# A down piece between the fourth and fifth seven-product pair, and third sums written over the raw words

## The chip, the cores and the metric

The kernel runs on one core of one Trainium2 chip. The metric is the device time of one execution in microseconds (us); lower is better. Engines are named as in the profile: PE (TensorE matmul), PEld (its weight load), DVE (VectorE), ACT (ScalarE), POOL (GpSimd) and SP (the queue that issues the loads here).

## The reference, cut to what matters

Two post-norm residual layers over 256 tokens of width 2048. Each layer has a mixer and a SwiGLU with 5632 hidden columns; the change lies in the SwiGLU alone.

```python
def swiglu(x, w_gate, w_up, w_down):
    return (jax.nn.silu(x @ w_gate) * (x @ w_up)) @ w_down
...
    for layer in range(DEPTH):
        ...
        x = layer_norm(DN_ALPHA * x + y, ln_mix_g[layer], ln_mix_b[layer])
        f = swiglu(x, ffn_w_gate[layer], ffn_w_up[layer], ffn_w_down[layer])
        x = layer_norm(DN_ALPHA * x + f, ln_ffn_g[layer], ln_ffn_b[layer])
```

## The kernel before

**Products.** Every float32 operand is split into a high part (a cast to float32r on ACT) and a low part (a subtraction on DVE); `mm3` then does three matmuls: low x high, high x high, high x low. The tokens are two tiles of 128. A matmul here is 128x128 times 128x512.

**SwiGLU.** The hidden columns are 11 chunks of 512. Chunks 0 and 1 are done by `whole`, the other nine by `unit`, so there are 9 units in a layer and 18 in all. For a unit, each of 8 weight pairs `w[p]` holds four blocks of 128x512 (two of gate, two of up). The four results of a unit, `c11`, `c12`, `c21`, `c22` (gate and up of the two token tiles), stand in four PSUM banks with the tag `un`.

- Three of the pairs (0, 1, 2) are multiplied plainly: two halves of 12 matmuls each.
- Five pairs (`SEVEN` = 3 to 7) are multiplied with seven block products in place of eight. Their left sides (`forms`, made once for a layer by `forms_of`) and their right sides are sums of blocks. `load_seven` loads a pair's four blocks as one 1 MB transfer into `raw` (tag `rs`, two buffers), makes two sums with the fourth block (the one operation that writes `z`), a third sum, and a fourth sum (`ze`, in a place called `room`), and splits block 0 and the first three sums into `sh` (high) and `sl` (low), two buffers each. A pair's four products at this stage are 12 matmuls.

**Order of a unit on PE.** It is written out by hand and pinned. First the unit before is finished: two "flips", each four transposes of one token tile of its result. Then the five seven-product pairs (`BEGIN` names the products and the results they go to), with `run(gap)` after each. Then ACT and DVE rework the four banks (the lines with `g0` and `g1` in `unit`: `c11` is copied, three differences are taken on DVE, and `c21` is written back by ACT with its sign changed). Then the remaining products, in the order `ORDER`: for pairs 3 to 7 three products each with `load_half` and the split of `edge` (`zf`); for pairs 0 to 2 two halves each. The first of these pieces is that of pair 3: three matmuls into `c11`, three into `c12`, three into `c21`.

**Down pieces.** `down_steps` is a generator of the down projection of two finished chunks. One step is one `load_half` (512 KB) and 12 matmuls into banks `acc`. A unit runs eight steps: in the kernel before, one ahead of each flip and one behind the second, then `GAPS` = 1, 1, 1, 0, 2 behind the five pairs.

**Order of everything else.** On DVE, ACT and the SP queue a scheduler decides at build time, from priorities (`tc.high_priority`) and its own estimates, in which order the instructions stand; each engine then runs its list in that order. Buffers: `whi`, `wlo` and `raw` of `load_half` have four each; `rs`, `sh`, `sl` have two each. A load into `rs` therefore waits until every reader of the pair two before has finished, and a cast into `sh` waits until PE has finished with the pair two before.

The two lines of the whole that the prediction uses most:

```python
raw = sp.tile([P, 4, NCH], F32, tag="rs", name="rs", bufs=2)
hi = sp.tile([P, 4, NCH], F32R, tag="sh", name="sh", bufs=2)
```

Of the kernel before, what the change touches and what calls it, by code (L numbers as in the profile page):

```python
# [11 lines left out]
F32 = mybir.dt.float32  # L12
# [6 lines left out]
P = 128  # L19
# [4 lines left out]
NCH = 512  # L24
# [46 lines left out]
ROUNDS = (((2, 3), (0, 1)), ((4, 5), (2, 3)), ((6, 7), (4, 5)), ((8, 9), (6, 7)), ((10,), (8,)))  # L71
LAST = (9, 10)
SEVEN = (3, 4, 5, 6, 7)
GAPS = (1, 1, 1, 0, 2)
ORDER = (3, 0, 4, 5, 1, 6, 7, 2)


# [1 line left out]
def trunk(ctx: ExitStack, tc: tile.TileContext, a, out):  # L79
    nc = tc.nc  # L80
    mult, add, sub = ALU.mult, ALU.add, ALU.subtract
# [15 lines left out]
    def bank(tag, bufs):  # L97
        return banks["pool"].tile([P, NCH], F32, tag=tag, name=tag, bufs=bufs)
# [22 lines left out]
    def split(hi, lo, src):  # L121
        nc.scalar.copy(hi, src)  # L122
        return nc.vector.tensor_tensor(lo, src, hi.bitcast(F32), op=sub).ins  # L123
# [53 lines left out]
    def half_done(n=1):  # L177
        for entry in list(later):
            entry[0] -= n
            if entry[0] <= 0:  # L180
                later.remove(entry)
                entry[1]()
# [95 lines left out]
    def split_tile(pool, shape, src, tag, bufs=1):  # L278
        hi = pool.tile(shape, F32R, tag=tag + "h", name=tag + "h", bufs=bufs)
        lo = pool.tile(shape, F32R, tag=tag + "l", name=tag + "l", bufs=bufs)  # L280
        if src is not None:
            split(hi, lo, src)
        return hi, lo

    def mm3(o, lhs, rhs, start, stop, pin=False, **more):

        for n, (a, b) in enumerate(((1, 0), (0, 0), (0, 1))):
            ins = nc.tensor.matmul(o, lhs[a], rhs[b], start=start and n == 0, stop=stop and n == 2, **more)  # L288
            if pin:
                tc.keep_in_program_order(ins)  # L290

    def at(pair, *ix):
        return pair[0][ix], pair[1][ix]
# [110 lines left out]
    def forms_of(sp, xT, out, seven, tag):  # L404

        n = len(seven)
        xs = sp.tile([P, NT, 2 * n, P], F32, tag="rs", name="xs", bufs=2)
        fs = sp.tile([P, 4, n, P], F32, tag="z", name="fs", bufs=1)
        yield
        for t in range(NT):  # L410
            s = slice(2 * seven[0], 2 * seven[0] + 2 * n)
            nc.vector.tensor_tensor(xs[:, t], xT[0][t][:, s, :].bitcast(F32), xT[1][t][:, s, :].bitcast(F32), op=add)
            yield
        x11, x12, x21, x22 = (xs[:, t, e : 2 * n : 2, :] for t in range(2) for e in range(2))
        e, f, g, h = (fs[:, i] for i in range(4))
        nc.vector.tensor_tensor(e, x22, x21, op=sub)
        nc.vector.tensor_tensor(f, e, x11, op=add)
        yield
        nc.vector.tensor_tensor(g, x11, x21, op=sub)
        nc.vector.tensor_tensor(h, x12, f, op=sub)  # L420
        yield
        hi, lo = split_tile(sp, [P, 4, n, P], fs, tag)
        for i, p in enumerate(seven):
            x = lambda t, k: (xT[0][t][:, k, :], xT[1][t][:, k, :])
            e, f, g, h = (at((hi, lo), slice(None), j, i) for j in range(4))
            out[p] = {"11": x(0, 2 * p), "12": x(0, 2 * p + 1), "22": x(1, 2 * p + 1), "e": e, "f": f, "g": g, "h": h}

    def load_seven(sp, src, room):

        with tc.high_priority(offset=400):  # L430
            raw = sp.tile([P, 4, NCH], F32, tag="rs", name="rs", bufs=2)
            hi = sp.tile([P, 4, NCH], F32R, tag="sh", name="sh", bufs=2)
            lo = sp.tile([P, 4, NCH], F32R, tag="sl", name="sl", bufs=2)
            z = sp.tile([P, 3, NCH], F32, tag="z", name="z", bufs=1)
            ze = room
            last_load[0] = nc.sync.dma_start(raw, src).ins
            nc.scalar.copy(hi[:, 0], raw[:, 0])
            nc.vector.tensor_tensor(z[:, :2], raw[:, 0:3:2], raw[:, 3:4].to_broadcast([P, 2, NCH]), op=add)
            nc.vector.tensor_tensor(z[:, 2], z[:, 0], raw[:, 2], op=add)  # L439
            nc.vector.tensor_tensor(ze, z[:, 2], raw[:, 1], op=add)  # L440
            nc.vector.tensor_tensor(lo[:, 0], raw[:, 0], hi[:, 0].bitcast(F32), op=sub)
            split(hi[:, 1:], lo[:, 1:], z)
        return lambda i: (hi[:, i, :], lo[:, i, :]), ze


    BEGIN = ((0, "11", "c11"), (3, "f", "c12"), (1, "e", "c22"), (2, "g", "c21"))

    def unit(sp, w, lhs, forms, y, down, flips):


        def run(n):
            for _ in range(n):
                next(down, None)

        for _ in range(NT):
            run(1)
            flips.pop(0)()
        run(1)
        b = {n: bank("un", 4) for n in ("c11", "c12", "c22", "c21")}
        edge, room = {}, None  # L460
        for i, (p, gap) in enumerate(zip(SEVEN, GAPS)):
            if i % 2:
                room = ap_.tile([P, 4, T], F32R, tag=("y4h", "y4l")[i // 2], name="ze4", bufs=1)
                room = room.rearrange("p (e a) t -> p e (a t)", e=2).bitcast(F32)
            own = room[:, (i + 1) % 2] if i else sp.tile([P, NCH], F32, tag="ze", name="ze", bufs=1)
            wt, edge[p] = load_seven(sp, w[p], own)
            for j, x, name in BEGIN:
                mm3(b[name], forms[p][x], wt(j), i == 0, i == len(SEVEN) - 1, True)
            if i == len(SEVEN) - 1:
                with tc.high_priority(offset=1000):  # L470
                    g0, g1 = (sp.tile([P, NCH], F32, tag=n, name=n, bufs=1) for n in ("g0", "g1"))
                    nc.scalar.copy(g0, b["c11"])
                    nc.vector.tensor_tensor(g1, b["c12"], g0, op=sub)
                    nc.vector.tensor_tensor(b["c12"], g1, b["c22"], op=sub)
                    nc.vector.tensor_tensor(g1, g1, b["c21"], op=sub)
                    nc.scalar.activation(b["c21"], g1, AF.Copy, scale=-1.0)
                    nc.vector.tensor_tensor(b["c22"], g1, b["c22"], op=sub)
            run(gap)

        left = {n: 2 * (8 - len(SEVEN)) + (n != "c22") * len(SEVEN) for n in b}  # L480

        def product(name, x, wt):
            left[name] -= 1
            mm3(b[name], x, wt, False, left[name] == 0, True, skip_group_check=True)

        for p in ORDER:
            if p in SEVEN:
                hi, lo = load_half(w[p][:, 1:3])
                for i, x, name in ((0, "12", "c11"), (1, "h", "c12")):
                    product(name, forms[p][x], (hi[:, i, :], lo[:, i, :]))  # L490
                with tc.high_priority(offset=400):
                    ends = split_tile(sp, [P, NCH], edge[p], "zf", 2)
                product("c21", forms[p]["22"], ends)
                half_done()
                continue
            for n, ks in ((0, (2 * p, 2 * p + 1)), (1, (2 * p + 1, 2 * p))):
                hi, lo = load_half(w[p][:, 2 * n : 2 * n + 2])
                for tok in range(NT):
                    for kk in range(2):
                        product(f"c{tok + 1}{n + 1}", lhs(tok, ks[kk]), (hi[:, kk, :], lo[:, kk, :]))  # L500
                half_done()
        with tc.high_priority(offset=1000):
            for tok in range(NT):
                g = sp.tile([P, NCH], F32, tag=f"g{tok}", name=f"g{tok}", bufs=1)
                nc.scalar.activation(g, b[f"c{tok + 1}1"], AF.Silu)
                nc.vector.tensor_tensor(g, g, b[f"c{tok + 1}2"], op=mult)
                s = slice(tok * P, (tok + 1) * P)
                flips.append(lambda g=g, s=s: transpose4(g, y[0][:, :, s], y[1][:, :, s], 1000))
# [35 lines left out]
    def ffn(layer, xT, res, mix_pool, close_mix, keep, last):  # L544
# [35 lines left out]
        forms, making, sps, flips = {}, [], [], []  # L580
# [10 lines left out]
        def change_rooms():  # L591
            close_mix()
            sps.append(later_pool(stack, f"sp{layer}"))
            making.append(forms_of(sps[0], xT, forms, SEVEN[:3], "fm"))
            making.append(forms_of(sps[0], xT, forms, SEVEN[3:], "fn"))
            later.append([1, make])

        groups = {c: None for c in range(2)}
# [498 lines left out]
    xT = new_xT()  # L1097
# [11 lines left out]
    def later_pool(stack, name):  # L1109
        return stack.enter_context(tc.tile_pool(name=name, bufs=1, reuse_waits="tile"))  # L1110
# [22 lines left out]
    xT = layer_end(0, a["ab_out"], AB_OUT_GROUPS, yT, False)  # L1133
# [117 lines left out]
```

## Time and profile before

| what | value |
|---|---|
| median of 3 runs | 2186.45 us (2184.64 to 2187.55) |
| the profiled execution's own time | 2190.12 us |
| its span in the profile | 2187.8 us |
| granted TensorE clock, mean | 0.997 |
| PE busy | 2148.9 us (98%), 9910 matmuls |
| DVE busy | 1691.1 us (77%) |
| ACT busy | 1215.7 us (56%) |
| read from HBM | 463.94 MB, 213 GB/s over the span |

The profile is of one execution. Durations in it are those of single instructions; matmuls overlap, so the distance from one matmul's start to the next one's is what a matmul costs, not the duration shown. In rows of the timeline the first number is the start in us from the start of the span, the second the duration in us, then engine, line and operation, output and inputs, and in brackets the idle time of the engine ahead of the instruction with what ended it. The 18 units lie at about 605 to 1180 us and 1560 to 2135 us.

### The profile page before, as it was taken

To read this page: it belongs to the slowest core of one execution; us is meant where nothing else is said; L and a number is where in the kernel's file an instruction comes from. 1 tells how busy PE (TensorE), PEld (TensorE's weight loads), DVE (VectorE), ACT (ScalarE), POOL (GpSimd) and SP (SyncE) were. 2 spreads that over 40 slices of the span, in tenths; PEclk is the share of its full clock that TensorE was granted. 3 is DMA by queue.
4 is the path that set the end of the run, shared out by engine and by line. 5 is a ranking of instruction groups with operands and counts; after the bars stand their busy time and mean duration, and the time that the engine had idled before them with its cause. 6 is when DMAs were issued, how large, how long until landed. Compare 5 with 4: busy or idle time off the path is not lost.

```text
span 2187.8 us, 27113 instructions
## 1 busy us (share of the span) xinstructions
PE 2148.9 (98%) x9910; PEld 1778.7 (81%) x9910; DVE 1691.1 (77%) x2122; ACT 1215.7 (56%) x1580; POOL 37.5 (2%) x43
## 2 busy tenths in 40 slices
PE   9999999999999999999999999999999999999998
PEld 7888888888878888888888788888788888888876
DVE  6886688676698888888886776675988888888866
ACT  6445534555455566666565554454556666565653
POOL 0000001000000000000000000000000000000000
PEclk9999999999999999999999999999999999999999
DMA  8555545684666776776665663655776766676754
GB/s 293 161 163 182 167 132 189 194 286 143 211 232 241 240 242 238 251 242 220 238 220 194 214 217 121 212 178 174 266 245 239 250 239 219 244 236 244 241 165 172
DMA packets 118613, 467.82 MB, mean 214 GB/s; under 512 B 13904, under 2 KB 16976, under 8 KB 105680
## 3 DMA queue, kind: packets, MB, share of 16 engines
q1 hardware_dynamic: 118480, 466.09, 63.0%
q8 instruction: 78, 1.28, 0.2%
q14 instruction: 55, 0.45, 0.1%
HBM read 463.94 MB, written 2.10 MB: 213 GB/s over the span
## 4 chain that ended last, share of the span: by engine, by line
PE 92%; DVE 3%; ACT 3%; DMA 1%; issue 0%; SPq 0%; ACTq 0%; DVEq 0%
PE acc L288 52%; PE un L288 30%; PE mx L288 6%; PE mx L803 1%; DVE sl L123 1%; PE tr L119 1%; ACT whi L122 1%; ACT sh L122 1%; PE un L119 1%; DVE wlo L123 1%; DMA raw<-in_cd_in 0%; ACT res L541 0%; DVE res L326 0%; DMA raw<-in_ab_in 0%; PE mx L849 0%
## 5 line engine op out<-in xcount | busy, mean ns | idle before, releaser
L123 DVE TENSOR_TENSOR wlo<-raw,whi 128x1024 fp32r<-128x1024 f32 (+1 forms) x671 | 814.7, 1222 | 321.2 <-ACT whi L122 311.8
L122 ACT CAST whi<-raw 128x1024 fp32r<-128x1024 f32 (+1 forms) x671 | 702.6, 1050 | 587.5 <-PE acc L288 302.5
L288 PE MATMUL acc<-whi,yTl 128*128 128x512 f32 x832 | 329.0, 396 | 1.2 <-DVE g L568 1.1
L288 PE MATMUL acc<-whi,yTh 128*128 128x512 f32 x832 | 325.0, 391 | 0.0
L288 PE MATMUL acc<-wlo,yTh 128*128 128x512 f32 x832 | 324.3, 391 | 0.0
L288 PE MATMUL acc<-whi,xTl 128*128 128x512 f32 x800 | 318.4, 398 | 5.2 <-ACT whi L122 5.1
L288 PE MATMUL acc<-whi,xTh 128*128 128x512 f32 x800 | 315.2, 394 | 0.0
L288 PE MATMUL acc<-wlo,xTh 128*128 128x512 f32 x800 | 313.0, 394 | 0.1
L288 PE MATMUL un<-whi,xTh 128*128 128x512 f32 x522 | 203.1, 389 | 0.0
L288 PE MATMUL un<-wlo,xTh 128*128 128x512 f32 x522 | 203.1, 389 | 0.0
L288 PE MATMUL un<-whi,xTl 128*128 128x512 f32 x522 | 203.1, 389 | 0.0
L288 PEld LDWEIGHTS acc<-whi,yTl 128*128 128x128 f32 x832 | 156.6, 188 | 33.6 <-DVE g L568 1.5
L288 PEld LDWEIGHTS acc<-wlo,yTh 128*128 128x128 f32 x832 | 156.6, 188 | 33.3
L288 PEld LDWEIGHTS acc<-whi,yTh 128*128 128x128 f32 x832 | 156.8, 188 | 31.4
L123 DVE TENSOR_TENSOR sl<-z,sh 128x1536 fp32r<-128x1536 f32 x90 | 157.9, 1755 | 29.4 <-ACT sh L122 28.9
L288 PEld LDWEIGHTS acc<-whi,xTl 128*128 128x128 f32 x800 | 151.1, 189 | 35.7 <-ACT whi L122 6.5
L122 ACT CAST sh<-z 128x1536 fp32r<-128x1536 f32 x90 | 133.3, 1481 | 81.3 <-DVE z L439 81.3
L288 PEld LDWEIGHTS acc<-wlo,xTh 128*128 128x128 f32 x800 | 150.9, 189 | 31.5 <-DVE wlo L123 1.2
L288 PEld LDWEIGHTS acc<-whi,xTh 128*128 128x128 f32 x800 | 151.2, 189 | 28.8
L288 PEld LDWEIGHTS un<-whi,xTh 128*128 128x128 f32 x522 | 98.0, 188 | 20.4
L288 PEld LDWEIGHTS un<-whi,xTl 128*128 128x128 f32 x522 | 98.0, 188 | 20.3
L288 PEld LDWEIGHTS un<-wlo,xTh 128*128 128x128 f32 x522 | 98.0, 188 | 20.3
(270 smaller groups left out, 3025.6 us busy)
## 6 DMA issues: line engine op xcount, KB each, us to landing
raw<-in_gu SPq DMA_DIRECT2D x262, 512.0 KB, 4.6
rs<-in_gu SPq DMA_DIRECT2D x90, 1024.0 KB, 6.9
raw<-in_down SPq DMA_DIRECT2D x176, 512.0 KB, 4.3
raw<-in_ab_in SPq DMA_DIRECT2D x127, 512.0 KB, 4.1
raw<-in_cd_in SPq DMA_DIRECT2D x40, 512.0 KB, 4.5
raw<-in_ab_out SPq DMA_DIRECT2D x32, 512.0 KB, 4.6
raw<-in_cd_out SPq DMA_DIRECT2D x32, 512.0 KB, 4.2
bias<-in_na_bias SPq DMA_DIRECT2D x32, 64.0 KB, 4.0
```

What stands on the lines that cost most here:

```text
L119: return nc.tensor.transpose(o, src, eye)
L122: nc.scalar.copy(hi, src)
L123: return nc.vector.tensor_tensor(lo, src, hi.bitcast(F32), op=sub).ins
L288: ins = nc.tensor.matmul(o, lhs[a], rhs[b], start=start and n == 0, stop=stop and n == 2, **more)
L803: nc.tensor.matmul(m[:, 2 * h + s, :], kk[:, h, s * P : (s + 1) * P], qq[:, h, r * P : (r + 1) * P], start=True, stop=True,)
```

## The change

- `GAPS` becomes 1, 1, 1, 1, 2: a down piece stands between the fourth and the fifth pair. To keep eight pieces in a unit, the piece between the two flips goes: one piece, both flips, one piece, then the pairs.
- In `load_seven` the third sum is written over block 2 of `raw`, so `z` holds two sums and gets two buffers (before: three sums, one buffer). High and low parts are made in two operations of 1024 columns each, one from blocks 0 and 2 of `raw`, one from `z` (before: 512 columns from `raw` and 1536 from `z`). The order of the four blocks in `sh` and `sl` changes, and `BEGIN` with it; the products are the same. The fourth sum (`room`) is the last in the code.
- The forms are made in three groups of 2, 2 and 1 pairs (before: 3 and 2), and their sums `fs` share the two buffers of `z`.

```diff
-GAPS = (1, 1, 1, 0, 2)
+GAPS = (1, 1, 1, 1, 2)
...
-        fs = sp.tile([P, 4, n, P], F32, tag="z", name="fs", bufs=1)
+        fs = sp.tile([P, 4, n, P], F32, tag="z", name="fs", bufs=2)
...
-            z = sp.tile([P, 3, NCH], F32, tag="z", name="z", bufs=1)
-            ze = room
+            z = sp.tile([P, 2, NCH], F32, tag="z", name="z", bufs=2)
             last_load[0] = nc.sync.dma_start(raw, src).ins
-            nc.scalar.copy(hi[:, 0], raw[:, 0])
-            nc.vector.tensor_tensor(z[:, :2], raw[:, 0:3:2], raw[:, 3:4].to_broadcast([P, 2, NCH]), op=add)
-            nc.vector.tensor_tensor(z[:, 2], z[:, 0], raw[:, 2], op=add)
-            nc.vector.tensor_tensor(ze, z[:, 2], raw[:, 1], op=add)
-            nc.vector.tensor_tensor(lo[:, 0], raw[:, 0], hi[:, 0].bitcast(F32), op=sub)
-            split(hi[:, 1:], lo[:, 1:], z)
-        return lambda i: (hi[:, i, :], lo[:, i, :]), ze
+            nc.vector.tensor_tensor(z, raw[:, 0:3:2], raw[:, 3:4].to_broadcast([P, 2, NCH]), op=add)
+            nc.vector.tensor_tensor(raw[:, 2], z[:, 0], raw[:, 2], op=add)
+            split(hi[:, :2], lo[:, :2], raw[:, 0:3:2])
+            split(hi[:, 2:], lo[:, 2:], z)
+            nc.vector.tensor_tensor(room, raw[:, 2], raw[:, 1], op=add)
+        return lambda i: (hi[:, i, :], lo[:, i, :]), room
...
-    BEGIN = ((0, "11", "c11"), (3, "f", "c12"), (1, "e", "c22"), (2, "g", "c21"))
+    BEGIN = ((0, "11", "c11"), (1, "f", "c12"), (2, "e", "c22"), (3, "g", "c21"))
...
+        run(1)
         for _ in range(NT):
-            run(1)
             flips.pop(0)()
         run(1)
...
-            making.append(forms_of(sps[0], xT, forms, SEVEN[:3], "fm"))
-            making.append(forms_of(sps[0], xT, forms, SEVEN[3:], "fn"))
+            for n, e in enumerate((2, 4, 5)):
+                making.append(forms_of(sps[0], xT, forms, SEVEN[2 * n : e], f"f{n}"))
```

The built order of the instructions shows more than the diff. First DVE, at the end of the five pairs of one unit in the middle of layer 0, before. `z<-rs` is the first two sums of a pair, `z<-z,rs` its third sum, `ze` its fourth; `sl` are low parts; `g` and `un` are the rework of the four banks (numbers behind a name are buffer numbers; lines are two higher before than after).

```order
L438 TENSOR_TENSOR z<-rs 128x1024
L473 TENSOR_TENSOR g_7997<-un,g_7996 128x512
L439 TENSOR_TENSOR z<-z,rs 128x512
L474 TENSOR_TENSOR un<-g_7997,un 128x512
L440 TENSOR_TENSOR ze<-z,rs 128x512
L475 TENSOR_TENSOR g_7997<-g_7997,un 128x512
L123 TENSOR_TENSOR sl<-z,sh 128x1536
L477 TENSOR_TENSOR un<-g_7997,un 128x512
```

One other instruction stands between each two of the rework; all belong to the next unit's first pair. The same place on DVE after the change (rework: L471, L472, L473, L475):

```order
L436 TENSOR_TENSOR z<-rs 128x1024
L123 TENSOR_TENSOR wlo<-raw,whi 128x1024
L471 TENSOR_TENSOR g_8009<-un,g_8008 128x512
L437 TENSOR_TENSOR rs<-z,rs 128x512
L123 TENSOR_TENSOR sl<-z,sh 128x1024
L472 TENSOR_TENSOR un<-g_8009,un 128x512
L436 TENSOR_TENSOR z<-rs 128x1024
L123 TENSOR_TENSOR wlo<-raw,whi 128x1024
L123 TENSOR_TENSOR sl<-rs,sh 128x1024
L473 TENSOR_TENSOR g_8009<-g_8009,un 128x512
```

The first `z<-rs` now belongs to the next unit's second pair, the second one to its third pair, and the rework stands behind them; the next unit's first pair is done ahead of this piece.

Second, ACT at the same place, before: the copy of `c11` into `g`, casts, and L476, which writes `c21`.

```order
L472 COPY g_7996<-un 128x512
L122 CAST sh<-z 128x1536
L437 CAST sh<-rs 128x512
L122 CAST whi<-raw 128x1024
L476 ACTIVATE un<-g_7997 128x512
```

And after, from the copy (L470) to the write of `c21` (L474):

```order
L470 COPY g_8008<-un 128x512
L522 ACTIVATE acc<-res_3803 128x512
L122 CAST sh<-z 128x1024
L122 CAST whi<-raw 128x1024
L122 CAST sh<-rs 128x1024
L539 COPY res_3802<-acc 128x512
L522 ACTIVATE acc<-res_3802 128x512
L122 CAST whi<-raw 128x1024
L539 COPY res_3803<-acc 128x512
L122 CAST whi<-raw 128x1024
L522 ACTIVATE acc<-res_3803 128x512
L474 ACTIVATE un<-g_8009 128x512
```

Ten instructions stand between the two where there were three; the last `whi` cast ahead of L474 is that of a piece behind the first one of `ORDER`.

Third, PE at the start of a unit, before: the transposes of the first flip with matmuls of a down piece on both sides.

```order
L288 MATMUL acc<-wlo,yTh 128x512
L119 MATMUL un<-ident,g_7729 128x128 x4
L288 MATMUL acc<-whi,yTl 128x512
L288 MATMUL acc<-whi,yTh 128x512
L288 MATMUL acc<-wlo,yTh 128x512
```

And after: both flips stand together.

```order
L288 MATMUL acc<-wlo,yTh 128x512
L119 MATMUL un<-ident,g_7741 128x128 x4
L119 MATMUL un<-ident,g_7744 128x128 x4
L288 MATMUL acc<-whi,yTl 128x512
L288 MATMUL acc<-whi,yTh 128x512
```

## The prediction

> **What bounds the kernel now.** I read the page first, then the list of waits of PE, then the timeline of single engines at a unit, then the loads.
>
> ```profile
> span 2187.8 us, 27113 instructions
> PE 2148.9 (98%) x9910; PEld 1778.7 (81%) x9910; DVE 1691.1 (77%) x2122; ACT 1215.7 (56%) x1580; POOL 37.5 (2%) x43
> ...
> PE un L288 <- DVE sl L123: 14.0, 18, 1.2
> ...
> PE un L288 <- DVE yTl L123: 2.2, 3, 0.8
> ```
>
> PE is the bound, so only what PE waits for can be won. The largest wait comes 18 times, once in a unit. PE's timeline shows the place, a fifth pair in layer 0:
>
> ```profile
> 1018.59 0.39 PE L288 MATMUL un<-sh,fnl 128*128 128x512 f32 x1
> 1018.82 0.39 PE L288 MATMUL un<-sh,fnh 128*128 128x512 f32 x1
> 1019.94 0.50 PE L288 MATMUL un<-sl,fnh 128*128 128x512 f32 x1 [0.73 <-DVE sl L123]
> 1020.27 0.40 PE L288 MATMUL un<-sh,fnl 128*128 128x512 f32 x1
> ```
>
> A matmul normally starts 0.227 us after the one before (1018.59 to 1018.82). Here one starts 1.12 later, 0.89 late, and the next 0.33 later, 0.10 late: 1.0 us is lost to the pair's low part. DVE at that time, and its next work (first numbers are starts):
>
> ```profile
> 1002.22 0.69 DVE L441 TENSOR_TENSOR sl<-rs,sh 128x512 fp32r<-128x512 f32 x1 [1.06 <-ACT sh L437]
> ...
> 1013.31 1.22 DVE L438 TENSOR_TENSOR z<-rs 128x1024 f32<-128x1024 f32 x1
> ...
> 1015.05 0.68 DVE L439 TENSOR_TENSOR z<-z,rs 128x512 f32<-128x512 f32 x1
> 1016.26 1.23 DVE L123 TENSOR_TENSOR wlo<-raw,whi 128x1024 fp32r<-128x1024 f32 x1 [0.52 <-ACT whi L122]
> 1017.40 0.68 DVE L440 TENSOR_TENSOR ze<-z,rs 128x512 f32<-128x512 f32 x1
> 1018.12 1.76 DVE L123 TENSOR_TENSOR sl<-z,sh 128x1536 fp32r<-128x1536 f32 x1
> 1019.80 0.68 DVE L441 TENSOR_TENSOR sl<-rs,sh 128x512 fp32r<-128x512 f32 x1
> 1020.40 1.22 DVE L438 TENSOR_TENSOR z<-rs 128x1024 f32<-128x1024 f32 x1
> 1021.54 0.68 DVE L473 TENSOR_TENSOR g<-un,g 128x512 f32<-128x512 f32 x1
> 1022.14 0.68 DVE L439 TENSOR_TENSOR z<-z,rs 128x512 f32<-128x512 f32 x1
> 1022.74 0.69 DVE L474 TENSOR_TENSOR un<-g,un 128x512 f32<-128x512 f32 x1
> 1023.34 0.68 DVE L440 TENSOR_TENSOR ze<-z,rs 128x512 f32<-128x512 f32 x1
> 1023.94 0.68 DVE L475 TENSOR_TENSOR g<-g,un 128x512 f32<-128x512 f32 x1
> ```
>
> An operation of 1024 columns takes 1.22 and lets the next start after 1.14 (1020.40 to 1021.54), one of 512 takes 0.68 and 0.60. The rework L473 to L475 starts 1.7 us behind the end of the fifth pair's low part (1019.88) and is done in 3.1 us. What uses it last is the write of `c21` by ACT, and its user on PE:
>
> ```profile
> 1001.56 0.62 ACT L437 CAST sh<-rs 128x512 fp32r<-128x512 f32 x1 [1.67 <-PE un L288]
> ...
> 1025.22 1.05 ACT L122 CAST whi<-raw 128x1024 fp32r<-128x1024 f32 x1
> 1026.18 0.58 ACT L476 ACTIVATE un<-g 128x512 f32<-128x512 f32 x1
> ...
> 1028.48 0.39 PE L288 MATMUL un<-zfh,xTl 128*128 128x512 f32 x1
> ```
>
> `c21` is ready at 1026.76 and used at 1028.48, so 1.7 us of room are there now. The 1 MB loads of pairs, their landing (in us: least, median, most of 90), and two issues:
>
> ```profile
> rs<-in_gu SPq DMA_DIRECT2D x90, 1024.0 KB, 6.9
> DMA to landing us min/median/max: 4.7/6.9/8.9
> 1002.94 0.33 SPq L436 DMA_DIRECT2D rs<-in_gu  x1
> 1009.76 0.33 SPq L436 DMA_DIRECT2D rs<-in_gu  x1
> ```
>
> The load at 1002.94 is issued 0.03 us behind the end of the low part at 1002.22, the last reader of its buffer. It is that of the fifth pair, whose `z` starts at 1013.31: the 6.9 us of flight are hidden today.
>
> **The change, part by part.**
>
> *Piece behind the fourth pair.* It is 12 matmuls, 2.72 us, as the piece ahead of a flip shows, with what follows it:
>
> ```profile
> 989.75 0.39 PE L288 MATMUL acc<-whi,yTl 128*128 128x512 f32 x1
> ...
> 992.47 0.60 PE L119 MATMUL un<-ident,g 128*128 128x128 f32 x4
> 992.82 0.48 PE L288 MATMUL acc<-whi,yTl 128*128 128x512 f32 x1
> 993.14 0.39 PE L288 MATMUL acc<-whi,yTh 128*128 128x512 f32 x1
> ```
>
> The wait of 1.0 us goes; the sum below has the fifth pair's low parts ready 1.3 us early. The piece's own load, cast and subtraction stay; they only shift by one pair.
>
> *Flips together.* Behind each flip the second matmul comes 0.32 us after the first (992.82 to 993.14), 0.09 over the pitch; one of two such places goes, 0.1 us. `g` of both tiles and the two low parts `yTl` are ready ahead of their users with one piece between, so nothing is added. Gain in a unit: 1.1 us.
>
> *Same work, other widths.* DVE for a pair: 1.14 + 3 x 0.60 + 1.67 (1018.12 to 1019.80) = 4.6 before, 3 x 1.14 + 2 x 0.60 = 4.6 after. ACT: 0.62 + 1.48 before, 2 x 1.05 after. No term. The third group of forms adds a few operations of 0.4 to 1.2 us in `whole`, where DVE idles between weight pieces; if that cover failed it would cost up to 5 us in each layer, once. I take nothing.
>
> *Order on DVE.* This is the large term. The rework now stands behind the first sums (`z<-rs`) of the next unit's second and third pairs. DVE takes its list in order, so the rework waits for these loads to land. Why they are late follows from the two `rs` buffers. Let 0 be the end of the unit's first pair on PE:
>
> - The third pair's cast may now start (as at 1001.56): 1.05, and its low part 1.22: 2.3. That was the last reader of its `raw`, so the fifth pair's load is issued: + 6.9 = 9.2.
> - DVE from there: `z` 1.14, fourth pair's second low part 1.14, third sum 0.60, `wlo` 1.14, fourth sum 0.60, fifth pair's low part 1.14, `z` of the next first pair 1.14, fifth pair's other low part 1.22: 8.1, so 17.3. PE reaches the fifth pair at 7 x 2.72 = 19.0, so it does not wait there.
> - Only now is the fifth pair's `raw` free, and the next second pair's load is issued: + 6.9 = 24.2. DVE has finished the first pair's work at about 22 and stands still.
> - DVE then: `z` 1.14, `wlo` 1.14, L471 0.60, third sum 0.60, low part 1.14, L472 0.60, `z` 1.14 (the third pair's load has landed), `wlo` 1.14, low part 1.14, L473 0.68: 9.3, so 33.5; ACT writes `c21` with L474 in 0.6: 34.1. The bank `c12` is ready with L472, at 29.5.
>
> PE wants `c12` behind four pairs and six pieces, 10 x 2.72 = 27.2, and three matmuls of 0.227 into `c11`: at 27.9. It wants `c21` at 28.6. It waits 1.6, works 0.7, and waits again, 5.5 us in all. The bounds: with both flights at 4.7 the chain ends at 29.7 (1.1 late), with both at 8.9 at 38.1 (9.5 late). I take the median, since nothing here makes these loads special.
>
> This holds in the 16 units that have a next unit in their layer. In the last of each layer nothing stands between the rework, and 1.1 us is won. The start of the first units (PE waiting 2.2 us for `yTl` in the list above) may change by that much either way; I take nothing.
>
> *Clock.* A wait of 4 us in the middle of a unit is new to PE. These windows show a whole unit at full clock and what long waits did: the second and the fourth row are ahead of a drop of the granted clock (the column behind POOL):
>
> ```profile
> 954.90:1018.80 63.90, 63.17 (x282) 51.95 (x281) 53.86 (x58) 39.53 (x49) 0.00 (x0) 1.00 0.69 239
> ...
> 612.76:616.17 3.41, 1.82 (x8) 1.16 (x7) 3.41 (x5) 0.04 (x1) 0.00 (x0) 1.00 0.57 191
> 616.17:619.58 3.41, 3.41 (x10) 2.64 (x9) 2.38 (x3) 1.95 (x2) 0.00 (x0) 0.50 0.92 252
> 1237.40:1240.81 3.41, 1.41 (x9) 1.27 (x10) 3.41 (x6) 3.41 (x6) 0.00 (x0) 1.00 0.43 161
> 1240.82:1244.22 3.40, 3.40 (x12) 2.71 (x11) 2.67 (x4) 0.86 (x2) 0.00 (x0) 0.50 0.28 76
> ...
> 1239.40 0.63 PE L119 MATMUL tr<-ident,res 128*128 128x128 f32 x4 [2.78 <-DVE res L341]
> ```
>
> A window of 3.41 us in which PE was busy for 1.4 to 1.8 us was followed by one at half clock. Such a window costs up to 1.7 us; part of it falls into the wait, and half a microsecond comes back because DVE catches up with the later pieces. I take 1.0 in each of the 16 units, with 0 and 2 as ends. The Trainium skill says otherwise ("TensorE: Matmul & The Clock Gate", section "Why this matters for your kernels"): gaps should stay under some 3 us, and one whole idle window returns the clock to half. By it a wait of about 4 us would seldom hold a whole window; the traced drops came after 2.78 us and after two gaps of about 1 us, so here the trace is the stricter. By the rule alone the time would be that of the first rival below.
>
> *Sum.* 16 x (5.5 - 1.1 + 1.0) = 86, less 2 x 1.1 = 2: + 84 us. The profiled execution took 2190.1 with a span of 2187.8; 2190.1 + 84 = 2274. The median of the runs shown is 3.7 below that execution, so 2270.
>
> **The rivals.**
>
> 1. *The same wait at full clock.* Without the clock term: 16 x 4.4 - 2 = 68, so 2254. For it: the 1 us of waiting in a unit now left the clock at 1.00. Against it: the two drops above.
> 2. *The loads land sooner.* With both flights at 5.8, halfway to the least, PE waits 3.3: 16 x 2.2 - 2 = 33 us, 2219. For it: 4.7 does occur. Against it: half of 90 took over 6.9.
> 3. *Faster: the flights shrink under the point of balance.* PE's wait equals the 1.1 us gained when both flights are 4.7; under that, the change wins, and with 3 us for each all 18 units win 1.1 and it ends at 2166. At 4.4 each: 0.5 late, 16 x -0.6 - 2 = -12, so 2174. For it: DVE standing still lets fewer loads be in flight. Against it: not one of 90 was under 4.7. The Trainium skill ("DMA: Bandwidth & Descriptors", section "Anatomy of one DMA") fits a transfer, issued there from GpSimd, at 2.0 us and a share by bytes at 436 GB/s; for 1 MB I work out an estimate of 4.4 us, with which this rival's 2174 would come. The median of 6.9 beside other loads does not agree.
> 4. *Longer flights.* With 8.9, PE waits 9.5: 16 x 9.4 - 2 = 148 us with the clock term, 2334. Only if several loads queue at once.
>
> **How the numbers follow.** Forecast 0.45, rival 1 0.22, rival 2 0.15, rival 3 0.11, rival 4 0.07. The range leaves out rival 3's lower part and rival 4: 2205 to 2305; the forecast's own is 2255 to 2290. About 0.2% (4 us) is what a measurement of this kernel can tell from no change. Rival 3 gives 0.08 faster and 0.03 same; the rest, 0.89, is slower.
>
> **What would show it.** In the list of waits, "PE un <- DVE sl", 18 times, is gone. In its place PE waits in front of the first product into `c21` (`un<-zfh,xTl`), 16 times, for ACT L474, some 4 us each, and about 1.5 us for DVE L472. DVE's idle time ahead of `z<-rs` names the load `rs<-in_gu`, about 2 us each. Windows of half clock follow the waits. Wrong would I be if `z<-rs` of the second pair starts ahead of the fifth pair's last product, if flights were near 4.7, or if the waits of PE stayed under 1 us.

## The result, and the profile after

| | before | after |
|---|---|---|
| median of 4 runs each | 2185.55 us (2184.55 to 2187.55) | 2265.11 us (2263.7 to 2273.4) |
| ratio, 95% interval | | 1.0371 [1.0344, 1.0397] |
| profiled execution, its span | 2190.12, 2187.8 us | 2263.7, 2261.9 us |
| granted TensorE clock, mean | 0.997 | 0.984 |

The change costs 80 us by the medians, and 74 between the two profiled executions. The page of the changed kernel, its head:

```profile
span 2261.9 us, 27118 instructions
PE 2174.3 (96%) x9910; PEld 1798.8 (80%) x9910; DVE 1690.6 (75%) x2136; ACT 1220.1 (54%) x1582; POOL 38.0 (2%) x43
```

DVE and ACT do the same work as before (1690.6 against 1691.1 us, 1220.1 against 1215.7). PE has the same 9910 matmuls, is busy 25 us longer and idle 49 us longer. The list of waits (engine, line and operation that waits, what it waited for: total, times, longest):

```profile
DVE z L436 <- DMA rs<-in_gu: 78.3, 38, 5.2
...
PE un L288 <- ACT un L474: 50.4, 16, 3.9
...
ACT un L474 <- DVE g L473: 17.8, 17, 2.5
```

"PE un <- DVE sl", 14 us in 18 waits before, is gone. In its place PE waits for L474, the write of `c21`, in each of the 16 units that have a next unit in their layer, 3.15 us on average. One such unit in the middle of layer 0: PE first, then ACT, DVE and the SP queue.

```profile
1059.68 0.39 PE L288 MATMUL un<-wlo,f0h 128*128 128x512 f32 x1
1063.63 0.50 PE L288 MATMUL un<-zfh,xTl 128*128 128x512 f32 x1 [3.56 <-ACT un L474]
1063.96 0.39 PE L288 MATMUL un<-zfh,xTh 128*128 128x512 f32 x1
```

```profile
1058.86 1.04 ACT L122 CAST whi<-raw 128x1024 fp32r<-128x1024 f32 x1
1059.80 0.57 ACT L539 COPY res<-acc 128x512 f32<-128x512 f32 x1
1060.27 1.05 ACT L122 CAST whi<-raw 128x1024 fp32r<-128x1024 f32 x1
1061.22 0.60 ACT L522 ACTIVATE acc<-res 128x512 f32<-128x512 f32 x1
1062.98 0.60 ACT L474 ACTIVATE un<-g 128x512 f32<-128x512 f32 x1 [1.16 <-DVE g L473]
```

```profile
1051.94 1.22 DVE L436 TENSOR_TENSOR z<-rs 128x1024 f32<-128x1024 f32 x1
...
1054.21 0.68 DVE L471 TENSOR_TENSOR g<-un,g 128x512 f32<-128x512 f32 x1
...
1056.55 0.69 DVE L472 TENSOR_TENSOR un<-g,un 128x512 f32<-128x512 f32 x1
1058.85 1.23 DVE L436 TENSOR_TENSOR z<-rs 128x1024 f32<-128x1024 f32 x1 [1.61 <-DMA rs<-in_gu]
1059.99 1.22 DVE L123 TENSOR_TENSOR wlo<-raw,whi 128x1024 fp32r<-128x1024 f32 x1
1061.13 1.22 DVE L123 TENSOR_TENSOR sl<-rs,sh 128x1024 fp32r<-128x1024 f32 x1
1062.26 0.68 DVE L473 TENSOR_TENSOR g<-g,un 128x512 f32<-128x512 f32 x1
```

```profile
1047.12 0.33 SPq L435 DMA_DIRECT2D rs<-in_gu  x1
...
1052.05 0.33 SPq L435 DMA_DIRECT2D rs<-in_gu  x1
```

Read backwards: the product into `c21` waits for L474, ACT stood idle ahead of L474 for DVE's L473, and L473 stands behind the `z<-rs` of the next unit's third pair, whose load was issued at 1052.05 and for which DVE stood still 1.61 us. The second pair's `z<-rs` (1051.94) did not wait: its load was issued 4.8 us earlier. In all 16 units L473 stands behind these two sums; the wait for the load differs: in 14 of them DVE stood still for the third pair's load, 0.4 to 1.7 us, 1.2 on average. In the first unit of each layer it waited for neither load, and PE still waited 3.9 and 2.2 us for `c21`.

Where the 74 us of span went, by the distance from the first transposes of one unit to those of the next: the 14 units in the middle of a layer take 67.65 us on average instead of 63.89 (+53 in all), and the two first units 78.1 and 76.5 instead of 68.2 and 65.2 (+21). Ahead of the first unit stand +1.7 us, between the layers and at the end together -1.4.

### The profile page after: what moved, and what is told of

Read it like the earlier page. It is cut to its first block, busy times and chain, and to the rows that moved or that the text cites. A ratio compares the mean times of both kernels' runs of the same rounds, so it can differ in the third digit from the quotient of the medians.

```text
span 2261.9 us, 27118 instructions
## 1 busy us (share of the span) xinstructions
PE 2174.3 (96%) x9910; PEld 1798.8 (80%) x9910; DVE 1690.6 (75%) x2136; ACT 1220.1 (54%) x1582; POOL 38.0 (2%) x43
## 4 chain that ended last, share of the span: by engine, by line
PE 87%; DVE 5%; DMA 4%; ACT 2%; issue 1%; SPq 0%; DVEq 0%; ACTq 0%
PE acc L288 48%; PE un L288 31%; PE mx L288 4%; DMA rs<-in_gu 3%; PE mx L801 1%; DVE wlo L123 1%; DVE sl L123 1%; PE tr L119 1%; DMA raw<-in_down 1%; ACT whi L122 1%; PE un L119 1%; ACT un L474 0%; DVE g L473 0%; DMA raw<-in_cd_in 0%; DVE z L436 0%
## 5 line engine op out<-in xcount | busy, mean ns | idle before, releaser
L288 PE MATMUL un<-whi,xTl 128*128 128x512 f32 x522 | 211.6, 405 | 0.0
L288 PE MATMUL un<-wlo,xTh 128*128 128x512 f32 x522 | 211.3, 405 | 0.0
L288 PE MATMUL un<-whi,xTh 128*128 128x512 f32 x522 | 210.9, 404 | 0.0
L436 DVE TENSOR_TENSOR z<-rs 128x1024 f32<-128x1024 f32 x90 | 110.0, 1222 | 78.5 <-DMA rs<-in_gu 78.3
L123 DVE TENSOR_TENSOR sl<-rs,sh 128x1024 fp32r<-128x1024 f32 x90 | 110.0, 1222 | 54.3 <-ACT sh L122 54.3
L122 ACT CAST sh<-rs 128x1024 fp32r<-128x1024 f32 x90 | 94.7, 1052 | 72.5 <-PE un L288 68.5
L122 ACT CAST sh<-z 128x1024 fp32r<-128x1024 f32 x90 | 94.8, 1053 | 63.5 <-PE un L288 53.4
L288 PEld LDWEIGHTS un<-whi,xTl 128*128 128x128 f32 x522 | 103.5, 198 | 22.6
```

The costliest lines, as they stand in the source:

```text
L436: nc.vector.tensor_tensor(z, raw[:, 0:3:2], raw[:, 3:4].to_broadcast([P, 2, NCH]), op=add)
```

## Experiments

Theory: DVE's list is the cause, the rework of the banks standing behind sums whose loads come late. Rival A: the moved piece itself leaves too little time ahead of `c21`. Rival B: ACT's list, where the write of `c21` stands behind casts, copies and seeds of other work. The times of before beside these runs are medians of 2186.8, 2186.9 and 2188.4 us.

**The piece and the flips alone**, on the old loading of pairs:

```diff
-GAPS = (1, 1, 1, 0, 2)
+GAPS = (1, 1, 1, 1, 2)
...
+        run(1)
         for _ in range(NT):
-            run(1)
             flips.pop(0)()
```

> Only the moved down piece and the flips together, on the old loading of pairs (raw words, forming in L434 to L443 as before). Theory (order on VectorE: with the new sums the rework of the banks stands behind the z<-rs sums of the next unit's second and third pair, whose transfers come late): the old loading has the rework elsewhere, so the wait for the write of c21 is absent or under 1 us in each unit, and the wait of 1.0 us before the fifth pair is gone: 2165 us (2155 to 2182). Rival A (the piece itself is what costs: behind the fourth pair it leaves too little time between the last pair and the products that need c21): the 3 to 4 us wait for the write of c21 is here too, and the time is 2240 us or more.

Measured: 2171.72 us, ratio 0.9935 [0.992, 0.995]: faster. Its first waits of PE, and the one for the write of `c21` (here L476):

```profile
PE un L288 <- DVE yTl L123: 5.0, 2, 2.8
PE acc L288 <- ACT whi L122: 4.8, 1, 4.8
...
PE un L288 <- ACT un L476: 0.9, 2, 0.5
```

No wait for `c21` but twice, no wait ahead of the fifth pair, and a middle unit takes 62.87 us, 1.0 less than before. Rival A falls: on the old loading the moved piece wins 15 us.

**The new sums alone**: the changed kernel with `GAPS` and the flips as before.

> Only the new third sums, the two operations of 1024 columns and the forms in three groups; the down piece stays behind the fifth pair and the flips stay apart. Theory (order on VectorE): the rework stands behind late sums here too, but PE has one more piece of 5.5 us between the last pair and c21, so the wait is smaller than the 3.3 us of the changed kernel, and some units fall to half clock: 2225 us (2195 to 2250). Rival A (the piece's place alone): no wait for c21, 2185 us within 5.

Measured: 2256.63 us, 1.0321 [1.0305, 1.0336]. The sums alone cost 70 us, more than either theory gave them. The expectation also had an error: the piece that moved does not lie between the last pair and `c21`, where two pieces stand in both kernels, so there was no reason for a smaller wait. The moved piece, worth 15 us on the old loading, costs 8 us beside the new sums: 2256.63 us without it, 2265.11 with it. There is little left for it to win, since the new sums alone already bring PE's waits for the low parts `sl` from 14.0 us in 18 waits to 1.4 in 3. Of the 9.7 us between the two profiled spans about 7 lie in the two first units and 4 in the middle ones (67.38 and 67.65 us).

```profile
PE un L288 <- ACT un L474: 47.4, 16, 3.3
```

In one of its units DVE had finished L473 long before ACT wrote:

```profile
1054.78 0.68 DVE L473 TENSOR_TENSOR g<-g,un 128x512 f32<-128x512 f32 x1
```

```profile
1054.67 1.05 ACT L122 CAST whi<-raw 128x1024 fp32r<-128x1024 f32 x1 [0.24 <-PE acc L288]
...
1057.58 1.04 ACT L122 CAST whi<-raw 128x1024 fp32r<-128x1024 f32 x1
1058.53 0.60 ACT L474 ACTIVATE un<-g 128x512 f32<-128x512 f32 x1
```

So in this version rival B's list is the one that ends last: 3.1 us pass between the end of L473 and the write, with ACT at work on other things. It is so in all 16 units: ACT comes to the write straight from other work, and L473 ends 1.2 to 3.1 us before it. Was it the casts? **The same with ACT's casts held** behind the write of `c21`:

```diff
-                hi, lo = load_half(w[p][:, 1:3])
+                with ExitStack() as order:
+                    if p != ORDER[0]:
+                        order.enter_context(tc.issue_after(rework[1]))
+                    hi, lo = load_half(w[p][:, 1:3])
```

(`rework` holds the last DVE operation of the rework and ACT's write of `c21`.)

> The new sums without the moved piece (as the run with the sums alone), and ScalarE's casts of the later products issued behind the write of c21; VectorE's order at the rework as in that run. In its trace VectorE had finished L473 at 1055.46 and the write began only at 1058.53, ScalarE being busy all the time with two casts of later products, a seed, a copy and a cast of the next second pair. Theory (in this version ScalarE's list is the limit): without the two casts, 0.95 each, the write starts about 1.9 us earlier, the wait falls from 3.0 to about 1.1 us with less half clock: 2207 us (2190 to 2222). Rival (VectorE's list is the limit here too): no change, 2256 us (2248 to 2264).

Measured: 2222.34 us, 1.0149 [1.0132, 1.0166]; the wait went from 47.4 to 26.3 us in 16 units. ACT's list is the limit here, as the theory said, though less came back than the 1.9 us a unit that two casts take; the copy, the seeds and the cast of the next pair still stand ahead of the write.

**ACT's casts held in the changed kernel** (the same edit):

> The changed kernel with ScalarE's order alone altered: the casts of the products behind ORDER's first pair are issued behind the write of c21. The order on VectorE is untouched. Theory (VectorE): the write of c21 already stood idle for 1.16 us for VectorE's L473 in the changed kernel, so it begins at most 0.2 us earlier: 2265 us (2250 to 2280; above 2265 if the casts now come late). Rival B (ScalarE: the write stands behind the casts and seeds): the wait of 3.3 us falls below 1 us and the time to 2195 us (2180 to 2215).

Measured: 2265.21 us, 1.0356 [1.0341, 1.0371], against 2265.11 for the changed kernel: nothing.

```profile
PE un L288 <- ACT un L476: 52.9, 16, 4.6
```

```profile
1058.83 0.60 ACT L528 ACTIVATE acc<-res 128x512 f32<-128x512 f32 x1
1061.41 0.60 ACT L476 ACTIVATE un<-g 128x512 f32<-128x512 f32 x1 [1.97 <-DVE g L475]
```

ACT is free 2.4 us earlier in this unit and stands idle for DVE, as it does in all 16 (2.0 to 4.0 us). With the piece moved, DVE's list is the first limit, as the theory had it.

**The rework in one piece on DVE**, ahead of the sums of the next second and third pair:

```diff
+                if rework and i in (1, 2):
+                    order.enter_context(tc.issue_after(rework[0]))
+                wt, edge[p] = load_seven(sp, w[p], own)
```

> The changed kernel with one edit: the sums of the next unit's second and third pair are issued behind the last operation of the rework, so that on VectorE the rework stands in one piece ahead of both. Theory (VectorE): no wait for c21 and no half clock behind it, 16 units at about 63 us: 2180 us (2165 to 2195), the two first units of the layers still some 15 us longer than before. Rival B (ScalarE's casts and seeds ahead of the write): the write still comes 2 us or more late, 2230 us or more. Rival A (the piece's place): c21 is needed before the rework can be done even in one piece, 2230 us or more.

Measured: 2195.80 us, 1.0041 [1.0028, 1.0053]; 69 of the 80 us are back, and the wait for `c21` is gone from PE's list, which now begins so:

```profile
PE un L288 <- DVE yTl L123: 7.0, 2, 4.3
PE un L119 <- DVE g L510: 5.8, 9, 1.2
PE acc L288 <- ACT whi L122: 4.8, 1, 4.8
```

In this kernel's built order ACT's write also moved ahead of copies and casts, so it shows the rework's place and not DVE alone. The next two take it apart.

**The third pair's sum alone held behind the rework** (`i == 2` in the edit above); ACT's order unchanged:

> The changed kernel with the hold on the third pair alone: its sum z<-rs is issued behind the rework, the second pair's stays ahead of it; ScalarE's order as in the changed kernel. Theory (VectorE alone sets the write of c21): L473 comes about 2.7 us earlier (1.61 of waiting for the load and 1.14 of the sum), the wait of PE falls below 1 us and the time to about 2200 us. Theory (two limits: VectorE, and behind it ScalarE, whose copies, seeds and casts ahead of the write end at 1061.8 in the unit shown, where the write began at 1062.98): the wait shrinks only from 3.3 to about 2.2 us, half clock still follows in many units, 2250 us (2232 to 2262).

Measured: 2235.75 us, 1.0221 [1.0199, 1.0244]. The wait is 38.1 us in 16 units, 2.4 each, near the 2.2 of the theory with two limits:

```profile
PE un L288 <- ACT un L479: 38.1, 16, 3.1
```

```profile
1047.17 0.68 DVE L478 TENSOR_TENSOR g<-g,un 128x512 f32<-128x512 f32 x1
...
1047.92 1.04 ACT L122 CAST whi<-raw 128x1024 fp32r<-128x1024 f32 x1
1048.87 0.60 ACT L528 ACTIVATE acc<-res 128x512 f32<-128x512 f32 x1
1049.40 0.59 ACT L479 ACTIVATE un<-g 128x512 f32<-128x512 f32 x1
```

DVE is done at 1047.85 and the write begins 1.55 us later, straight behind ACT's own work. Two limits stand one behind the other. **Both held**, the third pair's sum on DVE and the casts on ACT:

> The changed kernel with both: the third pair's sum behind the rework on VectorE, and the casts of the later products behind the write of c21 on ScalarE. The second pair's sum stays ahead of the rework. Theory (two limits, third pair only): the wait for the write of c21 falls below 0.5 us, 2197 us (2185 to 2210). If the second pair's sum ahead of the rework costs too, as the prediction's chain had it, a wait of 1.5 us or more stays in each of 16 units: 2225 us or more.

Measured: 2207.14 us, 1.0092 [1.007, 1.0113]; a wait of 15.6 us in 16 units is left, between the two expectations: 0.7 to 1.0 in the middle units, 2.8 and 2.1 in the two first. In a middle unit the two lists now end together, DVE's L478 at 1038.41 and ACT's work ahead of the write at 1038.36:

```profile
1037.73 0.68 DVE L478 TENSOR_TENSOR g<-g,un 128x512 f32<-128x512 f32 x1
```

```profile
1037.76 0.60 ACT L531 ACTIVATE acc<-res 128x512 f32<-128x512 f32 x1
1038.44 0.60 ACT L479 ACTIVATE un<-g 128x512 f32<-128x512 f32 x1
```

With the second pair's sum behind the rework as well, as in the run with the rework in one piece, the rest of the wait is gone and the time falls by another 11 us; by the profiles, 12 us apart, 7 lie in the two first units and 5 in the 14 middle ones. So the way back from 2265 us has three steps: 29 us for the third pair's sum on DVE, 29 more for ACT's casts, 11 for the second pair's sum, this last beside an order on ACT that was built anew too. The hold on the casts brought nothing in the changed kernel and 29 us beside the hold on DVE: DVE's list had hidden ACT's.

**The first units.** In the trace of the piece alone, the flips' low parts `yTl` of a layer's first unit stand behind the second pair's sums. The second pair's loading was put behind them:

```diff
+                if first and i == 1:
+                    order.enter_context(tc.issue_after(turned))
```

> The moved piece and the flips alone (old loading of pairs), and in the first unit of each layer the loading of the second pair is issued behind the low parts yTl of the flips. Theory (in the first units the flips' low parts stand behind the second pair's sums on VectorE, which costs PE 2.8 and 2.2 us and half clock behind it): both waits fall to 1 us or less, 2166 us (2160 to 2171). Rival (the second pair then comes as much later as the flips come earlier): 2171 us (2168 to 2178).

Measured: 2184.48 us, 0.9986 [0.9975, 0.9997], 13 us slower than without it; neither number was right, the sign was the rival's. The waits for `yTl` are gone and later, larger ones for the second pair have come:

```profile
PE un L288 <- ACT sh L122: 6.6, 4, 2.9
...
PE un L288 <- DVE sl L123: 4.6, 4, 1.2
```

**The same hold beside the rework in one piece:**

> The changed kernel with the rework in one piece ahead of the next unit's second and third pair, and in the first unit of each layer the second pair's loading behind the flips' low parts. Theory: the first units, 8.8 and 9.8 us over the others with the first hold alone, fall to 4 us over them: 2185 us (2178 to 2192). Rival (they are long for another reason, such as the forms made beside them): 2194 us (2190 to 2200).

Measured: 2185.20 us, 0.9987 [0.9973, 1.0001]. The first units shrank, from 71.6 and 72.6 to 69.0 and 68.1 us, and the middle units grew from 63.48 to 63.95, which cancels it; with a hold, the order behind it is built anew too. What the profiled span won, 6 us, lies between the layers (4.7) and ahead of the first unit (1.7), so that the theory's number was met but not by its sum. With all of the waits for `c21` mended the new sums still only reach the kernel before; the piece alone is 13 us better. The version that beats both kernels is the first of these runs.

Two things stay open. How much of the third pair's share is its load and how much the sum itself was not tried apart; the two first units, late without a wait for a load, show that the place alone can be enough. And why the rework in one piece is 24 us slower than the piece alone is only placed, by distances: 10 us in the two first units, 9 in the middle ones of layer 1, 5 between the layers.

## Why the prediction was right, point by point

The forecast was 2270 us, within 2205 to 2305; 2265 was measured. Direction, place and cause were right: the rework stands in DVE's list behind sums that wait for loads, and PE waits for the write of `c21` in 16 units. The chain that gave the size did not run as forecast, two of the prediction's own three signs of being wrong came true, and the nearness of the number is in part luck.

- *Piece behind the fourth pair, flips together: -1.1 a unit.* Right in size: alone they bring a middle unit from 63.89 to 62.87, 1.0 us. But the new sums take most of that wait away without the piece.
- *Same work, no term.* Right for the busy times. The step had no word on what the new sums do to order, but the next one had.
- *Order on DVE: a wait of 5.5 us in 16 units.* The place, the count of 16 and the cause were right: the rework in one piece gives 69 of the 80 us back. The size is the mis-sized term. By the list it is 3.15, by the distances of the matmuls' starts 3.45 with what the second one loses.
  - The fifth pair's and the next second pair's loads were put at the median flight of 6.9, "since nothing here makes these loads special", which made `c12` late. It was not: in the unit shown `z<-rs` of the second pair started at 1051.94 without a wait, and PE's list has no wait for L472. It started ahead of the fifth pair's last product, as in 14 of the 16 units, and that was a sign of being wrong:

```profile
1052.89 0.39 PE L288 MATMUL un<-sl,f2h 128*128 128x512 f32 x1
```

  Flights near 4.7 were another such sign. Over all 90 loads the median fell from 6.9 to 5.0, and it hides that a flight goes by the load's place in the unit: after the change the median is 4.8 for the first, second and fifth pair, 6.35 for the third and 7.0 for the fourth. So both flights of the chain were 4.8. Before the change one place stood out already, the third pair with 4.8 beside 6.3 to 7.6.

```profile
rs<-in_gu SPq DMA_DIRECT2D x90, 1024.0 KB, 5.0
DMA to landing us min/median/max: 4.6/5.0/8.0
```

  - The third pair's load was taken as landed. It was the one waited for, 1.61 us in the unit shown, and the sum behind it stands ahead of L473. With 4.8 for its two flights the prediction's chain leaves a wait of 1.3 us, near its point of balance; the wait for the third pair's load adds 1.2 on average, and some 1 us more is not assigned. So the size came near because a load left out made up for two that were put too long.
  - ACT's list did not appear in the chain as a limit. It is a second one, 1.2 us behind DVE's in the unit shown (ACT is free at 1061.82, L474 starts at 1062.98) and 0.8 on average over the 16; its order was known from the built kernel and not priced. It hid what mending the third pair alone would have brought.
- *Last units win 1.1.* Not told apart from what lies beside them.
- *First units: nothing.* Wrong by 14 us. They grew by 9.9 and 11.3 us where the middle units grew by 3.8. The waits in them:

```profile
PE un L288 <- DVE yTl L123: 9.6, 2, 6.4
...
PE un L119 <- DVE g L566: 4.4, 3, 2.2
```

  The prediction saw the 2.2 us for `yTl` before and gave them a change of that size either way. In layer 0 a sum that waits for its load came to stand between the two low parts, as it did in the rework:

```profile
618.13 1.23 DVE L436 TENSOR_TENSOR z<-rs 128x1024 f32<-128x1024 f32 x1 [2.33 <-DMA rs<-in_gu]
619.27 0.68 DVE L123 TENSOR_TENSOR yTl<-un,yTh 128x512 fp32r<-128x512 f32 x1
```

- *Clock: 1.0 in each of 16 units.* A middle unit takes 67.65 against 62.87 us with the piece alone; less the wait of 3.45 that leaves 1.3. Fourteen of the sixteen waits were followed by a window at half clock. In the middle units it comes out unit by unit: the same difference is 1.3 to 1.6 us in the 12 with such a window and under 0.1 in the two without. The windows (length, busy time of PE, PEld, DVE, ACT, POOL with counts, granted clock, DMA share, GB/s) of the unit shown, and of one of the two waits that were not:

```profile
1061.49:1064.90 3.41, 1.27 (x6) 1.06 (x7) 3.41 (x5) 1.44 (x3) 0.00 (x0) 1.00 0.50 159
1064.90:1068.31 3.41, 3.41 (x10) 2.63 (x9) 3.38 (x5) 0.12 (x1) 0.00 (x0) 0.50 0.58 177
...
1976.26:1979.67 3.41, 1.98 (x9) 1.31 (x7) 3.21 (x3) 3.38 (x6) 0.00 (x0) 1.00 0.06 23
1979.67:1983.08 3.41, 1.84 (x8) 1.52 (x9) 3.41 (x5) 1.54 (x3) 0.00 (x0) 1.00 0.49 154
1983.08:1986.49 3.41, 3.41 (x17) 2.81 (x16) 3.38 (x6) 1.06 (x1) 0.00 (x0) 1.00 0.84 234
```

  In the second case a gap of 3.0 us fell across a window's edge, with 1.4 to 1.6 us idle on each side, and the clock stayed. So the first rival (the same wait at full clock, 2254) fell. The Trainium skill ("TensorE: Matmul & The Clock Gate", section "Why this matters for your kernels") asks for one idle window ahead of the drop; the trace does not agree, since 2.14 of 3.41 us idle were enough.
- *The sum.* Per middle unit 5.4 us were forecast and 3.76 measured, 26 us less over 16; the first units, put at nothing, gave back 14 beyond that and the stretch ahead of them 1.7. That 2270 came so near to 2265 is in part luck: a term that was too large met places that the sum had put at nothing.

The second rival, loads that land sooner, came nearest to the wait's size (3.3 us, at flights of 5.8), though the real chain was another: short flights, late third pair. The third, faster, had its point of balance at flights of 4.7; the two flights that it speaks of came to 4.8 and the kernel was still far from faster, since the third pair's load, which flew 6.35, stood in the list too.

## What to carry to other kernels

An instruction's place in the list that an engine works through in order is part of its cost: sums that leave DVE's and ACT's busy times alone cost 70 us by themselves and 80 with the moved piece, because the reworking of a result came to stand behind other work, on ACT behind casts, copies and seeds, on DVE behind sums that wait for a load. After an edit to one stage, look at what now stands ahead of the last writer of what PE uses next, on each engine of that chain, since a second engine's list may hold the same place 1 us behind. Try the halves of a change apart, and do not add them up: here one was worth -15 us, the other +70, and both together +80. And price a load by its own place in the stage, not by the median of all its kind.

## What the runs showed of the hardware

- The clock falls after a window of 3.41 us that is only partly idle. The half-clock stretches of a trace start on a grid of 3.41 us. Cut on that grid, the windows ahead of the 14 drops in the changed kernel's units held 0.05 to 1.34 us of PE work as the profile models it, and the windows on both sides of the two gaps without a drop held 1.82 to 2.23. Over the eleven traces of this case every window at full clock with up to 1.52 us of PE work was followed by one at half clock (91), and with 1.55 or more only two were, at 1.80 and 1.83, the latter in the kernel before. A gap of 3 us is dear or free by where it falls.
- The same 1 MB loads took a median of 5.0 us in place of 6.9; with the rework in one piece it was 6.2, with the piece alone 6.8. The rate over the span does not explain it: with both lists held the median was 4.9 at 211 GB/s, with the rework in one piece 6.2 at 212. By place in the unit the medians run from 4.8 to 7.0 in the changed kernel; what sets them was not tried. A flight's length is a result of the schedule as much as an input to it.
